# Merge units' maxima copied a slot later, the second weight sum in the next slot, weights asked for ahead of attention loads, and conv work paced by other counts

## The chip, the cores and the metric

The kernel runs on one core of a Trainium2 chip. Time is the device time of one execution in microseconds (us). The engines are TensorE (PE: matmuls and transposes; PEld are its weight loads), VectorE (DVE), ScalarE (ACT), GpSimd (POOL) and SyncE (SP), which here issues nearly all DMAs. Each engine works through its own queue in order and waits on semaphores for the others.

## What is computed

One decoder layer in float32 with a convolution branch and an attention branch, for x of 2048 tokens and 1024 channels. The attention has 12 heads of 128 channels in three dilated window groups, and four outputs are merged over the groups by a softmax of their log denominators.

```python
z = h @ w_in                                  # h: normalised x, 1024 -> 9728 columns
a, b, g_conv, q, k, v, g_attn, m_conv, m_attn = jnp.split(z, SPLIT_POINTS, axis=-1)
u = a * jax.nn.sigmoid(b)
u = depthwise_causal_conv(u, conv_w, conv_b)  # 31 taps
u = jax.nn.silu(layer_norm(u, conv_ln_w, conv_ln_b)) * jax.nn.silu(g_conv)
y_conv = u @ w_conv_out
q = rope(rms_norm(q, q_norm_w), positions)
k = rope(rms_norm(k, k_norm_w), positions)
...
o = jnp.sum(wts[..., None] * o.astype(jnp.float32), axis=0)   # merge over the groups
y_attn = (o * jax.nn.silu(g_attn)) @ w_attn_out
y = jax.nn.sigmoid(m_conv) * y_conv + jax.nn.sigmoid(m_attn) * y_attn
x = x + gate[:, None] * (y @ w_out)
```

## The kernel before

**The big product.** h @ w_in takes most of the time. The matrices are cut into quarters, and seven products take the place of eight (`PRODUCTS`: B11, B21, T2, T1, T3, B22, T4). T1 to T4 are sums of weight quarters. Every float32 operand is split into a high and a low part (names S_hi/S_lo, shT/slT, shB/slB: h is the high part, l the low one), and a product of four 128-row pieces is 4 x 3 = 12 matmuls. Such a product is a *slot*; its twelve matmuls follow each other every 0.23 us, 2.7 us together, while TensorE doesn't wait.

**The loop over slots** (L1597 on) does all of the work of the two token halves: first Q, K and V columns of half 0, then its gate columns, then the same for half 1 (`half_jobs`). In each slot it runs its agenda in a set order: enter, load, act, pe, vec, (prepare), act2, the product itself (with "mid" inside it), tail, store. TensorE's instructions stand in the order in which this loop writes them. DVE, ACT, POOL and SP stand so too in the stages of Q, K and V; from a few slots after the last V turn until the next half a scheduler orders them.

**Weights.** `column_steps` (L267 to L305): `load` asks for a weight quarter by a DMA on SP (L271), `combine` makes a sum on POOL (L276; T2 into a new tile wT2), `split` writes the high part on ACT (L281) and the low part on POOL or DVE (L282), and in half 0 it stores the sums T to DRAM (L287) for half 1, which loads them again. `prepare(s + AHEAD)` runs a split three slots ahead of its product, `ask(s + AHEAD + 2)` the loads five slots ahead.

**Rotation of K and Q.** After a K or Q column its sum of squares is taken (sqk, pssk, prqk), the inverse root is computed as a power on POOL (stk, L707: a tile of 128x16), set on ACT (L719) and finished on POOL (L723); TensorE spreads it over a matmul (pwk, L727), DVE makes rwk of it, and TensorE makes rsk (L736), which DVE multiplies in.

**Attention units.** `unit()` (L820 to L968) returns the steps of two query blocks with the slot in which each runs, counted from its scores: loads of q, k and v at -3 (`load`, L841 to L856, with "pkv", the earlier half's keys and values, where a unit crosses into it), the fetch of the merge's earlier partial sums at -1 under "store" in half 1 and at -2 under "load" in half 0 (L873), scores at 0, exponents at 1 (L901), the turn of the probabilities at 2 (ptp, then the copy pT by DVE in half 1 and by ACT in half 0, L913 to L915), weights of the merge at 3, values (po, L938), the output osb, its turn (pta, L959) at 5 and its store (L965) at 6. Units of group 0 (named 8_, 9_, 10_ and 11_ for the four heads) merge: they copy the other groups' maxima and sums into stm (POOL, L903), take the minimum (DVE), the exponents on ACT (L919) and DVE's products of them. The tags of the loads have few buffers: "x" (pkv and part) three, pT one.

**Conv work.** The 31-tap convolution runs on DVE in single steps (ce, cq) which the loop's end slips in as long as a credit lasts: each slot adds PACE for its stage and takes away `spent`, an estimate of what DVE was given in this slot (`Counted`, L206). All DVE instructions that go through `vec` bear the line L210. At the end of this loop "later" work of the start (xl, xs) is slipped in the same way.

## Time and profile before

| | us |
|---|---|
| three runs | 2369.66, 2358.53, 2369.1 |
| median | 2369.1 |
| the profiled execution | 2367.32 |
| its span | 2365.1 |

The profiled execution's mean granted TensorE clock was 0.992. How to read the views: a page's first part gives busy time, share of the span and number of instructions for each engine. Busy time by stretch gives, for each, its length, then busy time and instructions of PE, PEld, DVE, ACT and POOL, then the clock, the share of DMA and GB/s. The waits give who waited for whom, the total, the times and the longest. A timeline row is start, duration, engine, line, operation, and in brackets the idle time ahead of it and what ended it. Rows of groups give the line, engine, operation, out<-in, the shapes, the count, and the busy time and mean ns of one. Buffer numbers are left out of names there.

The stages on this clock: start-up to 65 us, Q, K and V of half 0 from there to about 290, attention of half 0 beside them and beside the gates to about 660, gates of half 0 to 960, Q, K and V of half 1 to 1470 with attention from 1130, its rest to 1580, gates of half 1 and the two output projections to 2365.

### The profile page before, as it was taken

How to read it: one execution, taken by the hardware profiler on the slowest of the kernel's cores; microseconds unless marked ns; L12 is line 12 of the kernel's file. 1: busy time of each engine (PE TensorE's matmuls, PEld its weight loads, DVE VectorE, ACT ScalarE, POOL GpSimd, SP SyncE). 2: the span in 40 equal slices, each digit the busy share in tenths (PEclk: the TensorE clock that was granted, in tenths of full speed). 3: DMA queues.
4: the chain of work that ended last, by engine and by line, in shares of the span. 5: the costliest groups of instructions: out<-in, count | busy, mean ns of one | idle time of the engine just before them, and what ended most of it. 6: DMA issues, size and time to landing. Idle time of an engine off the chain costs nothing. (4 is left out here: it accounts for less than half of the span.)

```text
span 2365.1 us, 34440 instructions
## 1 busy us (share of the span) xinstructions
PE 2293.5 (97%) x11434; PEld 1866.9 (79%) x11434; DVE 1716.0 (73%) x2826; ACT 1106.4 (47%) x2255; POOL 1107.1 (47%) x866
## 2 busy tenths in 40 slices
PE   6999899999999999999999999999999999999999
PEld 4777688887778888787788887877888888888887
DVE  6668664567969789858757557699997957787544
ACT  4744455556644444644544445544444444332221
POOL 2345444445577789955333343445566630000221
PEclk9999999999999999999999999999999999999999
DMA  7666556666554454543666665645444579865553
GB/s 265 194 217 227 180 174 202 207 211 192 171 185 156 157 188 172 186 125 114 192 185 187 208 190 186 210 157 186 137 139 148 170 251 327 289 230 193 178 161 103
DMA packets 301226, 446.29 MB, mean 189 GB/s; under 512 B 28916, under 2 KB 132468, under 8 KB 301048
## 3 DMA queue, kind: packets, MB, share of 16 engines
q1 hardware_dynamic: 286776, 418.38, 55.7%
q10 hardware_dynamic: 14272, 25.72, 2.9%
q8 instruction: 90, 1.47, 0.3%
q14 instruction: 88, 0.72, 0.1%
HBM read 282.88 MB, written 161.09 MB: 188 GB/s over the span
## 5 line engine op out<-in xcount | busy, mean ns | idle before, releaser
L282 POOL TENSOR_TENSOR slT<-wT,shT 128x512 fp32r<-128x512 f32 x172 | 234.7, 1365 | 289.5 <-ACT shT L281 274.6
L282 POOL TENSOR_TENSOR slB<-wB,shB 128x512 fp32r<-128x512 f32 x152 | 202.8, 1335 | 160.5 <-ACT shB L281 146.5
L281 ACT ACTIVATE shB<-wB 128x512 fp32r<-128x512 f32 x222 | 139.8, 630 | 175.7 <-issue 34.0
L282 POOL TENSOR_TENSOR slT<-wB,shT 128x512 fp32r<-128x512 f32 x98 | 131.3, 1344 | 142.2 <-ACT shT L281 130.6
L210 DVE SCALAR_TENSOR_TENSOR ce<-us,pair_taps,ce 128x512 f32<-128x512 f32 x240 | 180.8, 753 | 6.2
L210 DVE SCALAR_TENSOR_TENSOR ce<-ut,chan,ce 128x512 f32<-128x512 f32 x240 | 179.4, 747 | 0.5
L281 ACT ACTIVATE shT<-wT 128x512 fp32r<-128x512 f32 x176 | 110.4, 627 | 128.3 <-PE paab L344 22.3
L210 DVE SCALAR_TENSOR_TENSOR cq<-ut,chan,cq 128x512 f32<-128x512 f32 x208 | 155.3, 747 | 4.0 <-ACT cq L411 4.0
L210 DVE CUSTOM_DVE_ANT_0 sm<-ps,mask,rqq 128x256 f32<-128x256 f32 (+1 forms) x192 | 78.0, 443 | 82.2 <-PE ps L879 37.2
L276 POOL TENSOR_TENSOR wB<-wB,wB 128x512 f32<-128x512 f32 x80 | 110.7, 1384 | 47.8 <-DVE slB L210 42.4
L281 ACT ACTIVATE shT<-wB 128x512 fp32r<-128x512 f32 x120 | 75.3, 627 | 67.5 <-PE paab L344 30.9
L938 PE MATMUL po<-v,pT 128*128 128x128 f32 x560 | 81.9, 277 | 4.1 <-ACT pT L915 3.7
L139 POOL TENSOR_SCALAR stf<-stf 128x4 f32<-128x4 f32 x4 | 1.7, 414 | 179.5 <-DVE stf L1716 142.5
L938 PEld LDWEIGHTS po<-v,pT 128*128 128x128 f32 x560 | 75.2, 191 | 11.4 <-ACT pT L915 4.6
L1888 ACT ACTIVATE yh<-yq 128x512 fp32r<-128x512 f32 x48 | 27.3, 622 | 119.4 <-POOL yq L1882 45.0
L210 DVE TENSOR_TENSOR slB<-wB,shB 128x512 fp32r<-128x512 f32 x70 | 58.6, 839 | 28.0 <-ACT shB L281 24.9
L901 ACT ACTIVATE sm<-sm,osb 128x256 f32<-128x256 f32 (+1 forms) x128 | 58.5, 462 | 10.5 <-DVE osb L210 6.4
L1879 POOL TENSOR_TENSOR ys<-yq 128x512 f32<-128x512 f32 x8 | 11.1, 1393 | 98.8 <-DMA yq<-y_d 98.8
L276 POOL TENSOR_TENSOR wT<-wB,wB 128x512 f32<-128x512 f32 x40 | 54.9, 1374 | 2.3
L910 PE MATMUL ptp<-ident,sm 128*128 128x128 f32 x332 | 52.4, 274 | 3.4 <-DVE stm L210 3.0
L1947 DVE TENSOR_TENSOR xt<-xt,oa 128x512 f32<-128x512 f32 x32 | 22.0, 687 | 45.9 <-PE oa L1960 45.9
L910 PEld LDWEIGHTS ptp<-ident,sm 128*128 128x128 f32 x332 | 41.1, 140 | 17.7 <-issue 5.2
(893 smaller groups left out, 7867.2 us busy)
## 6 DMA issues: line engine op xcount, KB each, us to landing
wB<-in_w_in_dram SPq DMA_DIRECT2D x262, 256.0 KB, 4.0
wT<-tT_d SPq DMA_DIRECT2D x136, 256.0 KB, 2.9
tT_d<-wB SPq DMA_DIRECT2D x102, 256.0 KB, 3.5
qk<-qk_d SPq DMA_DIRECT2D x96, 256.0 KB, 3.9
v_d<-vev SPq DMA_DIRECT2D x48, 256.0 KB, 3.7
qk_d<-spare_hi SPq DMA_DIRECT2D x48, 256.0 KB, 4.1
qk_d<-spare_lo SPq DMA_DIRECT2D x48, 256.0 KB, 4.3
v<-v_d SPq DMA_DIRECT2D x96, 128.0 KB, 3.7
```

What stands on the lines that cost most here:

```text
L139: nc.gpsimd.tensor_scalar(scratch, src, EPS, None, op0=ALU.add)
L210: return f(out, *args, **kw)
L276: nc.gpsimd.tensor_tensor(dst, x0, x1, op=ALU.subtract)
L281: nc.scalar.activation(h, q[name], AF.Copy)
L282: eng.tensor_tensor(l, q[name], h.bitcast(F32), op=ALU.subtract)
L901: nc.scalar.activation(sm[:, a:z], sm[:, a:z], AF.Exp, scale=-1.0, bias=box["low"][i], accum_out=box["total"][i])
L910: nc.tensor.transpose(pt[:, c : c + P], box["sm"][:, c : c + P], ident)
L938: nc.tensor.matmul(po[:, P * i : P * i + P], box["pT"][:, c : c + P], vt, start=(m == 0), stop=(m == count[i] - 1))
L1879: pool_tt(s1, a21, a22, op=ALU.add)
L1888: nc.scalar.activation(h, src, AF.Copy)
L1947: add = lambda dst, ps: tc.keep_in_program_order(nc.vector.tensor_tensor(dst, dst, ps, op=ALU.add))
```

## The change

- The minima and copies of a merge unit (POOL's copy, DVE's minimum) become steps of their own in slot 2 instead of slot 1, and the minimum counts 0.5 more in `spent`.
- T2 is summed in the step of the next product (n == 1) instead of in that of the first.
- In half 1 the probabilities' copy pT goes to ACT as long as the slot is not behind the last V turn, to DVE after it.
- The fetch of half 1 runs in slot -1 under "load" instead of under "store".
- `ask`, the weights' loads, comes ahead of the "load" agenda in each slot.
- The conv allowance: PACE is higher in three stages, each counted DVE instruction costs 0.14 instead of 0.12, the splits of quarters that land (`landed`) count 0.4 each, and an extra rest (AFTER) is added in gate stages once no attention unit is left.

```diff
--- before.py
+++ after.py
@@ -39,7 +39,7 @@
 WS, WR, AHEAD = 4, 10, 3
 QKV_LO = (((1, 3, 5), (1, 3, 5), (0, 1, 3, 5, 6)), ((), (), (1, 3, 5)))
 FIRST_GATES, BETWEEN = (1, 1), ((1, 2, 1, 2, 1, 2, 1, 3), (1, 1, 2, 1, 1, 2, 1, 4))
-PACE, AGAIN = (2.75, 3.05, 2.5, 2.85), 12
+PACE, AFTER, AGAIN = (2.87, 3.15, 2.62, 2.85), (0.75, 0.1), 12
 PLAIN_QK, LATER_END = 4, 65
 MANUAL, ORDER_END = (True, True), 6
 LATER_X = 20
@@ -206,7 +206,7 @@
                 size = 1
                 for d in out.shape[1:]:
                     size *= d
-                spent[0] += 0.12 + size / 860 * (1.3 if name == "tensor_tensor" else 1.0)
+                spent[0] += 0.14 + size / 860 * (1.3 if name == "tensor_tensor" else 1.0)
                 return f(out, *args, **kw)
 
             return call
@@ -298,6 +298,7 @@
             split(PRODUCTS[n][1], vec if n in lo_engines else nc.gpsimd)
             if fresh and n == 0:
                 combine("T1", q["B11"], q["B12"], q["B11"])
+            if fresh and n == 1:
                 combine("T2", None, q["B22"], q["T1"])
             if fresh and n == 2:
                 combine("T3", q["B12"], q["B22"], q["B12"])
@@ -899,9 +900,15 @@
             for i in range(2):
                 a, z = cols[i][0], 256 * i + 256
                 nc.scalar.activation(sm[:, a:z], sm[:, a:z], AF.Exp, scale=-1.0, bias=box["low"][i], accum_out=box["total"][i])
+
+        def lows():
             if g == 0:
                 nc.gpsimd.tensor_copy(box["st"][:, 0:2, :, 1:NG], box["part"][:, :, :, P:].rearrange("p i g k -> p k i g"))
+
+        def lowest():
+            if g == 0:
                 vec.tensor_reduce(box["st"][:, 4, :, 0:1], box["st"][:, 0], op=ALU.min, axis=AX.X)
+                spent[0] += 0.5
 
         def turn_p():
             pt = bank("o", f"ptp{n}")
@@ -909,7 +916,7 @@
                 for c in cols[i]:
                     nc.tensor.transpose(pt[:, c : c + P], box["sm"][:, c : c + P], ident)
             pT = box["pT"] = ap.tile([P, 512], F32, tag="pT", name=f"pT{n}", bufs=1)
-            if half:
+            if half and slot_now[0] > last_v[1]:
                 vec.tensor_copy(valid(pT), valid(pt))
             else:
                 nc.scalar.activation(valid(pT), valid(pt), AF.Copy)
@@ -964,10 +971,10 @@
             if g == 0:
                 nc.sync.dma_start(ai_d[h, :, P * j0 : P * j0 + 2 * P], box["asb"])
 
-        return ((-3, "load", load), ((-1, "store", fetch) if half else (-2, "load", fetch)), (0, "pe", scores), (1, "act", exps), (2, "tail", turn_p), (3, "act", weigh),
+        return ((-3, "load", load), ((-1, "load", fetch) if half else (-2, "load", fetch)), (0, "pe", scores), (1, "act", exps), (2, "act", lows), (2, "vec", lowest), (2, "tail", turn_p), (3, "act", weigh),
                 (3, "tail", values), (4, "store", keep), (5, "pe", turn_o), (6, "store", keep_o))
 
-    waiting, busy_until = [], [0]
+    waiting, busy_until, last_v = [], [0], {}
     slots_of = {}
 
     opened(rb, pool("rb"))
@@ -1532,6 +1539,7 @@
     at_slot(where_of[half_jobs][0] + AGAIN, rope_again, "enter")
 
     last_turn = [slots_of[h, V, 5][6] for h in range(2)]
+    last_v.update(enumerate(last_turn))
 
     def order_shut():
         if order:
@@ -1594,6 +1602,10 @@
         at_slot(s + 42 + i, lambda i=i: gate_sum(i), "pe")
     at_slot(s + 44, lambda: aside.pop("gp_c").__exit__(None, None, None))
 
+    def landed(name, k, raw):
+        quarter_split(1, name, k, raw, nc.gpsimd if k == 3 else vec)
+        spent[0] += 0.4 * (k < 3)
+
     credit = 0.0
     for s, (i, n) in enumerate(slots):
         run_agenda(s, "enter")
@@ -1605,8 +1617,8 @@
             if last_turn[half] and s > last_turn[half] + 8 and not waiting and s > busy_until[0]:
                 last_turn[half] = 0
                 attention_shut()
+        ask(s + AHEAD + 2)
         run_agenda(s, "load")
-        ask(s + AHEAD + 2)
         for where in ("act", "pe", "vec"):
             run_agenda(s, where)
         prepare(s + AHEAD)
@@ -1624,10 +1636,11 @@
         for name, k in asked[:2]:
             raw = gpa["p"].tile([P, 512], F32, tag="ai" if k == 3 else "gt", name=f"landing{name}_{k}", bufs=2 if k == 3 else 6)
             nc.sync.dma_start(raw, quarter_src(name, k))
-            held.append((s + 3, lambda name=name, k=k, raw=raw: quarter_split(1, name, k, raw, nc.gpsimd if k == 3 else vec)))
+            held.append((s + 3, lambda name=name, k=k, raw=raw: landed(name, k, raw)))
         del asked[:2]
         stage = (i >= gates_start[0]) + (i >= half_jobs) + (i >= gates_start[1])
-        credit = min(max(credit, -2.0) + PACE[stage] - spent[0], 2.0)
+        rest = AFTER[i >= half_jobs] if not waiting and s > busy_until[0] and stage % 2 else 0.0
+        credit = min(max(credit, -2.0) + PACE[stage] + rest - spent[0], 2.0)
         spent[0] = 0.0
         while credit > 0.35 and (conv_todo or later_todo and s >= later_from.get(later_todo[0][0], s + 1)):
             if conv_todo:
```

The order of TensorE's instructions is the same row by row in both kernels. Line numbers of the kernel after are one higher from L301 on, three at POOL's copy of a part (L906) and seven from ACT's pT (L922) on.

POOL in half 0, at the columns from 5632, where K unit 0_1 is rotated; before:

```order
L707 TENSOR_TENSOR stk0_1_1895<-stk0_1_1895,mhalf_128 128x16
L282 TENSOR_TENSOR slB11_0_5632_1902<-wB11_0_5632_1823,shB11_0_5632_1901 128x512
L276 TENSOR_TENSOR wB11_0_5632_1823<-wB12_0_5632_1827,wB11_0_5632_1823 128x512
L276 TENSOR_TENSOR wT2_0_5632_1906<-wB22_0_5632_1829,wB11_0_5632_1823 128x512
L723 TENSOR_TENSOR stk0_1_1895<-stk0_1_1895 128x2x8
L282 TENSOR_TENSOR slT4_0_4096_1949<-wB21_0_4096_1662,shT4_0_4096_1948 128x512
L282 TENSOR_TENSOR slT2_0_5632_2007<-wT2_0_5632_1906,shT2_0_5632_2006 128x512
```

and now:

```order
L708 TENSOR_TENSOR stk0_1_1897<-stk0_1_1897,mhalf_128 128x16
L282 TENSOR_TENSOR slB11_0_5632_1904<-wB11_0_5632_1824,shB11_0_5632_1903 128x512
L276 TENSOR_TENSOR wB11_0_5632_1824<-wB12_0_5632_1828,wB11_0_5632_1824 128x512
L724 TENSOR_TENSOR stk0_1_1897<-stk0_1_1897 128x2x8
L282 TENSOR_TENSOR slT4_0_4096_1948<-wB21_0_4096_1663,shT4_0_4096_1947 128x512
L276 TENSOR_TENSOR wT2_0_5632_1980<-wB22_0_5632_1830,wB11_0_5632_1824 128x512
L282 TENSOR_TENSOR slT2_0_5632_2007<-wT2_0_5632_1980,shT2_0_5632_2006 128x512
```

The sum wT2 moved from ahead of the last step for stk0_1 (L723, now L724) to behind it and behind the low part slT4 of the column before.

In half 1, at the columns from 5376, the sum stood ahead of the power for stk1_0 (L707); now it stands behind that, behind the low part slT4 of the column before and behind the last step for stk1_0.

SP, the DMA queue, near the end of half 1's attention (qk, v and pkv are loads of unit 11_1_x, part of a merge unit, wT and wB weights, ai_d a store); before:

```order
L873 DMA part10_1_4_14894<-acc2_d_89 128x2x260
L844 DMA qk11_1_0_14946<-qk11_d_74 128x2x256
L852 DMA pkv11_1_0_14950<-qk11_d_74 128x128
L856 DMA pkv11_1_0_14950<-v11_d_86 128x128
L271 DMA wT4_1_128_15276<-tT4_128_d_6163 128x512
L965 DMA ai_d_97<-asb10_1_0_14966 128x256
L271 DMA wB11_1_8704_15319<-in_w_in_dram 128x512
L845 DMA v11_1_0_14947<-v11_d_86 128x256
L844 DMA qk11_1_2_15041<-qk11_d_74 128x2x256
L844 DMA qk11_1_4_15134<-qk11_d_74 128x2x256
L271 DMA wB21_1_8704_15364<-in_w_in_dram 128x512
L873 DMA part10_1_6_14995<-acc2_d_89 128x2x260
```

and now:

```order
L874 DMA part10_1_4_14858<-acc2_d_89 128x2x260
L845 DMA qk11_1_0_14948<-qk11_d_74 128x2x256
L874 DMA part10_1_6_14946<-acc2_d_89 128x2x260
L271 DMA wT4_1_128_15269<-tT4_128_d_6158 128x512
L972 DMA ai_d_97<-asb10_1_0_14964 128x256
L271 DMA wB11_1_8704_15314<-in_w_in_dram 128x512
L846 DMA v11_1_0_14949<-v11_d_86 128x256
L845 DMA qk11_1_2_15042<-qk11_d_74 128x2x256
L845 DMA qk11_1_4_15133<-qk11_d_74 128x2x256
L271 DMA wB21_1_8704_15354<-in_w_in_dram 128x512
L853 DMA pkv11_1_0_14952<-qk11_d_74 128x128
L857 DMA pkv11_1_0_14952<-v11_d_86 128x128
```

part10_1_6 moved up by nine rows, and pkv11_1_0 down behind the weight wB21_1_8704.

DVE at merge unit 8_1_2 in the last V columns (its two rows TENSOR_REDUCE are the minimum and, later, a sum); before, the minimum stands 13 rows ahead of the first row shown here:

```order
L210 TENSOR_TENSOR spare_lo_170<-s1v1_5_13907,pbv1_5_14035 128x512
L210 COPY pT8_1_2_14063<-ptp8_1_2_14058 128x512
L210 TENSOR_TENSOR stm8_1_2_13920<-stm8_1_2_13920 128x6
L210 TENSOR_REDUCE stm8_1_2_13920<-stm8_1_2_13920 128x2
L210 RECIPROCAL stm8_1_2_13920<-stm8_1_2_13920 128x2
L210 SCALAR_TENSOR_TENSOR stm8_1_2_13920<-stm8_1_2_13920 128x6
```

and now:

```order
L210 TENSOR_REDUCE stm8_1_2_13919<-stm8_1_2_13919 128x2
L210 TENSOR_TENSOR spare_lo_170<-s1v1_5_13907,pbv1_5_14035 128x512
L210 TENSOR_TENSOR stm8_1_2_13919<-stm8_1_2_13919 128x6
L210 TENSOR_REDUCE stm8_1_2_13919<-stm8_1_2_13919 128x2
L210 RECIPROCAL stm8_1_2_13919<-stm8_1_2_13919 128x2
L210 SCALAR_TENSOR_TENSOR stm8_1_2_13919<-stm8_1_2_13919 128x6
```

The copy pT8_1_2 is gone (ACT has it), and the minimum stands one row ahead of the product that needs ACT's exponent of it.

## The prediction

> **What bounds the kernel now.** I read the page first (busy shares), then busy time by stage, then the waits of TensorE, then the timeline at each wait. The page says that TensorE is the bound, and that almost nothing is left:
>
> ```profile
> PE 2293.5 (97%) x11434; PEld 1866.9 (79%) x11434; DVE 1716.0 (73%) x2826; ACT 1106.4 (47%) x2255; POOL 1107.1 (47%) x866
> ```
>
> The view of windows says in which stage TensorE is idle (the first number is the length, the second PE's busy time):
>
> ```profile
> 200.00:290.00 90.00, 77.50 (x380) 59.26 (x379) 67.45 (x89) 36.09 (x69) 44.64 (x31) 0.94 0.57 179
> 290.00:535.00 245.00, 243.41 (x1419) 199.60 (x1418) 142.47 (x296) 135.49 (x360) 113.82 (x83) 1.00 0.64 196
> 535.00:665.00 130.00, 120.84 (x643) 101.08 (x642) 114.11 (x280) 76.92 (x202) 73.07 (x74) 1.00 0.58 190
> 665.00:960.00 295.00, 295.00 (x1304) 244.25 (x1303) 247.72 (x360) 139.81 (x241) 248.30 (x198) 1.00 0.49 170
> 960.00:1130.00 170.00, 161.85 (x770) 130.34 (x769) 125.09 (x140) 90.22 (x154) 113.20 (x77) 0.98 0.45 138
> 1130.00:1470.00 340.00, 331.64 (x1909) 275.74 (x1907) 217.48 (x418) 163.71 (x399) 124.69 (x95) 1.00 0.62 187
> 1470.00:1560.00 90.00, 86.08 (x446) 72.14 (x445) 62.46 (x172) 50.16 (x132) 36.46 (x41) 0.96 0.66 210
> 1560.00:1660.00 100.00, 96.51 (x433) 78.92 (x432) 93.41 (x148) 44.05 (x83) 56.11 (x42) 0.98 0.54 173
> 1660.00:2365.00 705.00, 701.03 (x3066) 569.97 (x3064) 512.35 (x756) 255.71 (x433) 219.50 (x169) 1.00 0.60 194
> ```
>
> Length less busy time: 12.50, 1.59, 9.16, 0, 8.15, 8.36, 3.92, 3.49 and 3.97 us, 51.1 us after 200 us. The change keeps TensorE's own order and work, so all it can gain is a part of these, and the matmul time lost at half clock. The waits behind them:
>
> ```profile
> PE pta L959 <- DVE osb L210: 4.0, 2, 2.8
> PE po L938 <- ACT pT L915: 3.7, 2, 2.6
> PE rsk L736 <- DVE rwk L210: 3.5, 2, 2.2
> PE ptp L910 <- DVE stm L210: 3.0, 2, 1.6
> PE po L938 <- DVE pT L210: 2.6, 4, 1.0
> PE pssk L687 <- ACT sqk L668: 2.4, 1, 2.4
> ```
>
> (total, times, longest; those for stk are shown below one by one). The half clock, in four short windows round 206 us and two round 247 us (the last three numbers: granted clock, DMA share, GB/s):
>
> ```profile
> 202.70:206.10 3.40, 0.36 (x2) 0.00 (x0) 3.40 (x4) 0.00 (x0) 3.32 (x3) 1.00 0.00 0
> 206.10:209.50 3.40, 3.28 (x9) 2.60 (x10) 2.99 (x3) 0.29 (x1) 1.78 (x2) 0.50 0.03 5
> 209.50:212.90 3.40, 2.11 (x9) 1.18 (x8) 2.54 (x4) 1.22 (x2) 0.00 (x0) 1.00 0.77 189
> 212.90:216.30 3.40, 3.40 (x9) 2.66 (x9) 3.40 (x6) 0.76 (x2) 0.00 (x0) 0.50 0.96 270
> 243.60:247.00 3.40, 0.93 (x18) 0.45 (x18) 3.35 (x5) 1.69 (x3) 0.00 (x0) 1.00 0.46 100
> 247.00:250.40 3.40, 3.40 (x9) 2.63 (x10) 0.26 (x1) 2.11 (x4) 1.70 (x2) 0.51 0.92 276
> ```
>
> A window in which TensorE was idle for 3.04, 1.29 or 2.47 of 3.40 us is followed by 3.4 us at clock 0.50. Half of that, 1.7 us, is lost on top of the wait, so a wait of 2 to 3 us is worth up to 4 to 5. The stage rows agree: a mean clock of 0.94 in 90 us is 5.4 us lost, three times 1.7 and a rest; 0.98 in 170 us (960 to 1130) is 3.4, 0.96 in 90 (1470 to 1560) 3.6, 0.98 in 100 (1560 to 1660) 2.0.
>
> **The change part by part.**
>
> *Second weight sum (T2) a slot later.* In several QKV columns T2 stood on POOL ahead of steps that TensorE was about to wait for:
>
> ```profile
> 203.95 1.59 POOL L276 TENSOR_TENSOR wT<-wB,wB 128x512 f32<-128x512 f32 x1
> 204.34 1.75 DVE L210 TENSOR_TENSOR slB<-wB,shB 128x512 fp32r<-128x512 f32 x1
> 205.50 0.67 POOL L723 TENSOR_TENSOR stk<-stk 128x16 fp32r<-128x16 f32 x1
> 206.22 0.40 PE L727 MATMUL pwk<-ident,stk 128*32 128x128 f32 x1 [3.16 <-POOL stk L723]
> 211.34 0.66 DVE L210 TENSOR_TENSOR rwk<-pwk,edge 32x512 fp32r<-32x512 f32 x1
> 212.06 0.73 PE L736 MATMUL rsk<-rwk,pick 32*128 32x512 f32 x2 [1.29 <-DVE rwk L210]
> 1081.94 1.61 POOL L276 TENSOR_TENSOR wT<-wB,wB 128x512 f32<-128x512 f32 x1
> 1088.81 0.28 PE L727 MATMUL pwk<-ident,stk 128*32 128x128 f32 x1 [3.34 <-POOL stk L723]
> ```
>
> Near 206 us: stk moves up by one sum, 1.59 us, so pwk's wait goes from 3.16 to about 1.6 us. What is late next is rsk, which waits for rwk on DVE; rwk stands behind an addition whose input is the product that TensorE finishes after pwk. That product ran at half clock. If the 3.4 us at 0.50 go too, it ends 1.6 + 1.7 us earlier, but DVE's queue gives back about 1 of that. I take -2.2 (from 0, if rsk's wait grows by all of it, to -3.3). Near 1089 us the same swap is worth 1.61, and of the 3.4 us that this stage loses to the clock I put half to this wait: -2.5 (0 to -3.3). T2's own readers are a product later, so its delay is hidden by one slot (2.7 us).
>
> The Trainium skill has a rule on this cover. Its page "SBUF — State Buffer", section "Who interferes with whom", says that a VectorE operation with both inputs in SBUF and a GpSimd operation that reads SBUF exclude each other. The trace agrees in kind: DVE's slB took 1.75 us beside the sum. By this rule T2, put later, slows other DVE operations, perhaps those ahead of rwk. That is a rival below, where its price comes from the rows.
>
> *DVE's early work near 225 to 266 us.* Two "later" additions move into a stretch in which DVE idles:
>
> ```profile
> 225.02 1.09 DVE L210 TENSOR_TENSOR spare_lo<-s1k,pbk 128x512 f32<-128x512 f32 x1 [3.18 <-PE pbk L344]
> ```
>
> One (xl123) used to stand behind this wait of 3.18 us and now stands ahead of it, so the chain of DVE operations that runs on without a gap up to 246 us is one operation shorter: 0.93 us with POOL beside it, 0.74 without. pssk's 2.4 us wait shrinks to about 1.6; the half clock after it may go. I take -1.6 (0 to -2.6), and -0.7 for the same move of xl113 before 266 us.
>
> *pT copied by ACT in half 1 up to the last V turn.* 36 copies leave DVE and go to ACT:
>
> ```profile
> L915 ACT ACTIVATE pT<-ptp x48: 377/490/598, 280.5 to 648.7; 128x384 f32<-128x384 f32 x20, 128x256 f32<-128x256 f32 x16, 128x512 f32<-128x512 f32 x12
> L210 DVE COPY pT<-ptp x48: 670/684/714, 1128.3 to 1573.9; 128x512 f32<-128x512 f32 x48
> ```
>
> (minimum, median, maximum in ns). 36 x 0.684 = 24.6 us leave DVE; 36 x 0.6 = 21.5 us (the full width is the maximum of ACT's row) come on ACT, which has 164 us to do in the 340 of this stage where DVE has 217. Half 0, which copies on ACT already, is the nearest row for what results: 1.59 us idle in 245. Scaled to 340 us that is 2.2, against 8.36 now: -6.2 at most. Units of half 1 that merge have more to do than those of half 0 in that row, so I take half, -3, about what the four waits for DVE's pT come to (2.6). The other end is +1: a pT that waits for its transpose holds up ACT's split of a weight behind it.
>
> *Merge.* In half 1 the fetch of a merge unit's part goes half a slot ahead, and its copy and minimum a slot back. One place has a visible stall:
>
> ```profile
> 1528.64 0.19 POOL L903 COPY stm<-part 128x8 f32<-128x8 f32 x1 [2.51 <-DMA part<-acc_d]
> 1528.87 0.16 DVE L210 TENSOR_REDUCE stm<-stm 128x2 f32<-128x6 f32 x1 [1.98 <-POOL stm L903]
> ```
>
> This part is now asked for right behind unit 11_1_0's load of queries and keys; before, five more loads, three weights and a store came first. So the 1.98 us go; the keys and values of the earlier half for unit 11_1_0 (pkv) take the late place, a risk that belongs to the +4 below. Behind them DVE has no gap until TensorE has waited for it (the rows of L910 and L959 are of this place in part): directly it gets at most those 1.98 us back, and the clock's 3.6 us of this stage go or stay. Its row bounds it, 3.92 idle and 3.6: -7.5 to 0. Two conv steps moved ahead of this place by the new allowance fill a part of the time that comes free:
>
> ```profile
> L210 DVE SCALAR_TENSOR_TENSOR ce<-us,pair_taps,ce 128x512 f32<-128x512 f32 x240 | 180.8, 753 | 6.2
> ```
>
> I take -3.5: 0.5 to 2 of the idle time and about half of the clock's loss. The waits of 1560 to 1660 us, behind weights' landing and DVE at 93%, stay as they are: 0, at most their 3.5 and 2.0.
>
> *Weights asked ahead of loads, and the allowance.* SP issues the same transfers, 112 of them at another place. What is queued behind a weight that waits for its buffer is now an attention load:
>
> ```profile
> SPq L271 <- POOL slT L282: 137.1, 76, 3.8
> SPq L852 <- PE po L938: 90.8, 24, 10.6
> qk<-qk_d SPq DMA_DIRECT2D x96, 256.0 KB, 3.9
> ```
>
> The longest such wait is 3.8 us. A load is issued three slots of 2.7 us ahead of its scores and lands in 3.9, so some 4 us of cover hide it: 0, with +4 as the far end (a load late by one full wait). In return the weights no longer stand behind loads that wait up to 10.6 us. The allowance rises by as much as the new prices take, and in the gate stages the order of DVE is nearly the same: 0. One conv step (0.75 us, the row above) moves ahead of a split near 975 us whose result TensorE waits for, a part of the 8.15 us idle there: +0.75. The 2.6 us wait for ACT's pT and the rest of the 9.16 us of 535 to 665 keep their order: 0.
>
> *Sum:* -2.2 - 2.5 - 1.6 - 0.7 - 3 - 3.5 + 0.75 = -12.75, say -12. The profiled run took 2367.3 us (its span 2365.1); it becomes about 2355. The median of the three runs is 1.8 higher, so against it 2357.
>
> The Trainium skill's page "TensorE: Matmul & The Clock Gate", section "Why this matters for your kernels", warns of TensorE gaps of over about 3 us between bursts. The trace differs: 1.29 us idle in the window from 209.5 were enough. By that rule only the two pwk waits would cost clock; without the clock's part in pssk's and the merge's terms, some 2.4 us, the time would be 2359.
>
> **The rivals.**
>
> 1. *Given back at the next wait.* rsk waits for rwk on DVE, at 212 us and once more for 2.2, whatever pwk does, and a T2 that now runs beside DVE's operations makes them 1.75 instead of about 0.7 us long. Then the two pwk terms come to -1 together, pssk's stays as it is, and the attention gives -3: -4, or 2365. For it: the row of rwk; that DVE is in a row of operations there. Against it: the half clock goes with the wait.
> 2. *More than the sum.* All of the clock losses named (5.4, 3.4 and 3.6) and some of the 8.36 us go, with the direct terms: -20, or 2349. For it: half 0's 1.59 us. Against it: each such gain needs the next engine to be early too.
> 3. *Slower: the merge's exponent becomes the wait.* With the minimum a slot later, ACT's exponent of the maxima and DVE's product of it stand right behind it, where a slot lay between them:
>
> ```profile
> L919 ACT ACTIVATE stm<-stm x64: 279/286/298, 524.1 to 1565.9; 128x3 f32<-128x3 f32 x64
> ```
>
> DVE then stands still for two of these, 0.57, and for what ACT has in hand, some 0.6: 1.2 us for each of the 32 merge units (two rows each). It decides from where DVE has no slack left to take it. If the 16 of half 1 and a quarter of the others pass it on, 20 x 1.2 = +24, less what the QKV stages gain (6): +18, or about 2387. Against it: DVE is busy in 64% of 1130 to 1470.
> 4. *Nothing.* The moves lie where TensorE does not wait, the allowance undoes itself: 2369. Against it: two of the moved sums stand right before the longest waits.
>
> **How the numbers follow.** My forecast 0.42; rival 1 0.27; rival 2 0.15; rival 3 0.10; rival 4 0.06. About 0.5% (11.8 us, below 2357.3 or above 2381) is what a measurement of this kernel can tell from no change; the forecast lies on that bound, so half of its chance counts as faster. Faster: 0.21 + 0.15 + a little of the ends, 0.40. Slower: 0.10. Same: 0.50. The range takes in rival 1, 4 and most of rival 2: 2345 to 2372.
>
> **What would show it.** Right: pwk's waits near 206 and 1089 us are about 1.6 us, and the windows after them are at clock 1.00; no "DVE pT" among TensorE's waits before 1470 us; DVE's minimum near 1528 us doesn't wait for POOL. Wrong: rsk's waits grow by as much; new rows of TensorE waiting for ACT (pT, spare_hi) or for a DMA; DVE's stm waiting for ACT's exponent at many merges.

## The result, and the profile after

Over 16 runs the changed kernel takes 2357.45 us in the median (2352.97 to 2363.04), the kernel before 2366.92 (2358.53 to 2372.91) over 16: a ratio of 0.9964, interval 0.9953 to 0.9974. By the ratio that is 8.5 us less (6 to 11), while the two medians are 9.5 apart: faster beyond the interval, and short of 0.5%. The profiled execution of the changed kernel is its fastest run, 2352.97 us with a span of 2350.7 and a mean granted clock of 0.996; that of before took 2367.32 at 0.992. The two profiles are 14.4 us apart, and this is more than the kernels are: how much of it is clock comes below.

The page's first row, and busy time by the same stretches of the clock as before, in which the work stands up to 11 us earlier now (length, busy time of PE, PEld, DVE, ACT, POOL, then clock, DMA share, GB/s):

```profile
PE 2286.3 (97%) x11434; PEld 1863.7 (79%) x11434; DVE 1692.9 (72%) x2790; ACT 1121.6 (48%) x2291; POOL 1108.3 (47%) x866
...
200.00:290.00 90.00, 77.66 (x393) 59.81 (x392) 67.56 (x90) 38.06 (x71) 45.47 (x31) 0.96 0.61 194
535.00:665.00 130.00, 122.42 (x641) 102.34 (x640) 114.56 (x280) 77.51 (x203) 72.00 (x71) 0.99 0.62 199
960.00:1130.00 170.00, 162.72 (x794) 131.51 (x793) 126.19 (x143) 89.55 (x155) 118.12 (x78) 1.00 0.45 141
1130.00:1470.00 340.00, 334.23 (x1930) 279.62 (x1929) 193.10 (x393) 183.69 (x447) 124.13 (x93) 1.00 0.64 191
1470.00:1560.00 90.00, 86.75 (x455) 72.94 (x454) 70.77 (x189) 50.36 (x133) 39.24 (x42) 0.98 0.60 193
1560.00:1660.00 100.00, 98.15 (x436) 80.30 (x435) 94.20 (x134) 43.66 (x77) 59.09 (x44) 1.00 0.59 185
```

TensorE's idle time went from 12.50 to 12.34, 9.16 to 7.58, 8.15 to 7.28, 8.36 to 5.77, 3.92 to 3.25 and 3.49 to 1.85 us. DVE lost 23 us of work and ACT gained 15, which is pT. The clock's means are higher in four of the six stages (0.04 x 90 us lost in the first stretch instead of 0.06 x 90, nothing between 960 and 1130 instead of 3.4) and lower in one, from 535 to 665.

The waits of TensorE (total, times, longest) show what took the place of what:

```profile
PE rsk L737 <- DVE rwk L210: 6.2, 3, 3.2
PE pwk L728 <- POOL stk L724: 4.3, 3, 1.8
PE pta L966 <- DVE osb L210: 4.0, 2, 2.8
PE ptp L917 <- DVE stm L210: 2.5, 2, 1.5
PE pssk L688 <- ACT sqk L669: 2.3, 1, 2.3
PE po L945 <- ACT pT L922: 2.1, 2, 1.2
```

The wait for stk fell from 6.9 to 4.3, but that for rwk rose from 3.5 to 6.2: together 10.4 and 10.5. Waits for DVE's pT, 2.6 before, are down to one late one of 0.4.

### The profile page after: what moved, and what is told of

The parts are those of the page before. It is cut to its first block, busy times and chain, and to the rows that moved or that the text cites. A ratio compares the mean times of both kernels' runs of the same rounds, so it can differ in the third digit from the quotient of the medians.

```text
span 2350.7 us, 34465 instructions
## 1 busy us (share of the span) xinstructions
PE 2286.3 (97%) x11434; PEld 1863.7 (79%) x11434; DVE 1692.9 (72%) x2790; ACT 1121.6 (48%) x2291; POOL 1108.3 (47%) x866
## 3 DMA queue, kind: packets, MB, share of 16 engines
q8 instruction: 90, 1.47, 0.2%
## 4 chain that ended last, share of the span: by engine, by line
PE 51%; DVE 3%; DMA 2%; ACT 1%; issue 1%; POOL 0%; SPq 0%; ACTq 0%; DVEq 0%; POOLq 0%
PE yc L1691 8%; PE oa L1973 4%; PE ya L1691 4%; PE paab L345 3%; PE pak L345 3%; PE pav L345 3%; PE paq L345 2%; PE oc L1973 2%; PE pag_g_d L345 2%; PE pag_ma_d L345 2%; PE pcab L345 2%; PE po L945 2%; PE pcv L345 1%; PE pcq L345 1%; PE pck L345 1%; DMA wg<-in_w_ada_dram 1%
## 5 line engine op out<-in xcount | busy, mean ns | idle before, releaser
L922 ACT ACTIVATE pT<-ptp 128x512 f32<-128x512 f32 (+2 forms) x84 | 44.8, 533 | 90.3 <-PE ptp L917 90.1
L276 POOL TENSOR_TENSOR wB<-wB,wT 128x512 f32<-128x512 f32 x40 | 54.9, 1373 | 0.0
```

The lines of the kernel that those rows point to most:

```text
L276: nc.gpsimd.tensor_tensor(dst, x0, x1, op=ALU.subtract)
L922: nc.scalar.activation(valid(pT), valid(pt), AF.Copy)
```

## The experiments

**How they are read.** "Undone" is the changed kernel with that one part put back, "alone" is the kernel before with that part put in. All kernels have TensorE's order of before, row by row. Medians of 6 to 12 runs tell differences of some 3 us, and most terms are smaller; so each is read at its place in the profile as well. The runs' times go with the clock: the 16 runs of the changed kernel reach from 2352.97 us at 0.996 to 2363.04 at 0.992 and 2362.87 at 0.991. The table therefore also has the mean over runs of time x granted clock, roughly what a run takes without the half clock (time that TensorE idles at half clock is taken off too, so it is no exact split).

| kernel | median us | ratio to before (interval) | mean clock | time x clock | of before, run beside it |
|---|---|---|---|---|---|
| changed | 2357.45 | 0.9964 (0.9953-0.9974) | 0.9938 | 2343.1 | |
| changed, again | 2359.09 | 0.9967 (0.9951-0.9982) | 0.9928 | 2341.8 | 2349.1 |
| before, again | 2367.64 | 1.0002 (0.9988-1.0016) | 0.9918 | 2348.1 | 2349.1 |
| T2 undone | 2358.94 | 0.9972 (0.9956-0.9988) | 0.9928 | 2342.5 | 2349.2 |
| pT undone | 2360.5 | 0.9975 (0.9959-0.9992) | 0.9931 | 2344.9 | 2349.2 |
| weights' place undone | 2363.66 | 0.9985 (0.9968-1.0001) | 0.9922 | 2346.1 | 2349.2 |
| later minimum undone | 2359.99 | 0.9976 (0.9963-0.9990) | 0.9923 | 2342.8 | 2349.2 |
| earlier fetch undone | 2359.91 | 0.9974 (0.9964-0.9984) | 0.9922 | 2341.8 | 2349.7 |
| allowance undone | 2359.43 | 0.9976 (0.9964-0.9989) | 0.9925 | 2342.5 | 2349.7 |
| T2 and weights alone | 2363.95 | 0.9981 (0.9967-0.9996) | 0.9935 | 2348.1 | 2349.7 |
| pT alone | 2362.16 | 0.9991 (0.9978-1.0004) | 0.9923 | 2345.5 | 2348.2 |
| rotary operations back, all K columns | 2370.16 | 1.0009 (0.9999-1.0019) | 0.9911 | 2348.4 | 2349.7 |
| rotary operations back, one column | 2360.9 | 0.9975 (0.9962-0.9989) | 0.9923 | 2342.5 | 2349.1 |

**T2 undone.**

```diff
             if fresh and n == 0:
                 combine("T1", q["B11"], q["B12"], q["B11"])
-            if fresh and n == 1:
                 combine("T2", None, q["B22"], q["T1"])
```

> The changed kernel with T2 summed again in the step of the first product; all else as changed. My theory (T2's place on POOL is what shortened the waits near 541 and 1084 us): TensorE's wait for stk near 1084 us is 2.7 to 3.4 us again instead of 1.06, the wait for ACT's pT near 541 us is 2.0 to 2.6 instead of 0.93, near 206 us the wait for stk is 3 us and that for rwk behind it shrinks from 3.18 to about 1.5, so that nothing is lost or won there; time 3 to 6 us above the changed kernel. Rival (the gain near 541 us comes from the merge's later minimum, not from T2): the wait near 541 us stays at about 0.9 and the time is 2 to 4 us above.

TensorE's timeline near 207, 213 and 1093 us (in brackets the wait):

```profile
207.39 0.29 PE L727 MATMUL pwk<-ident,stk 128*32 128x128 f32 x1 [3.44 <-POOL stk L723]
212.97 0.73 PE L736 MATMUL rsk<-rwk,pick 32*128 32x512 f32 x2 [0.95 <-DVE rwk L210]
...
1093.02 0.28 PE L727 MATMUL pwk<-ident,stk 128*32 128x128 f32 x1 [2.72 <-POOL stk L723]
```

Near 207 us the pair comes to 4.4 us; in the changed kernel it is 1.84 + 3.18 = 5.0. Near 1093 the wait is back to 2.72 from 1.06. The median rose by 1.5 us only, and time x clock not at all (2342.5 against 2343.1 and 2341.8): less than expected, and less than 1.7 us at one place, since the waits for DVE behind it shrink again (for rsk and the sums of Q, from 1.62 us together to 0.41). Some 0.45 us are left of it there, and T2's move takes nearly as much back near 488 us: TensorE waits 0.61 us for sums of Q in the changed kernel and in its repeat, 0.22 with T2 undone and in both profiles of the kernel before. Near 547 us the wait for pT came out at 3.8 us, which seemed to bear out that T2 matters there, but see the repeats.

**pT undone, and pT alone.** One edit, taken from the changed kernel or put into the one before:

```diff
-            if half and slot_now[0] > last_v[1]:
+            if half:
                 vec.tensor_copy(valid(pT), valid(pt))
```

> The changed kernel with half 1's pT copied by DVE throughout. My theory (these 36 copies are what DVE lost between 1130 and 1470 us, and the stage's gain of 4 us is theirs): TensorE's idle time between 1130 and 1470 us rises from 5.8 to 8 or 9 us, with waits for DVE's pT and for DVE's sqq near 1150 and 1430 us again; time 2.5 to 4 us above the changed kernel. Rival (the later minimum of the merge and the earlier weights did it): that stage stays at 5.8 to 6.5 us idle and the time within 1 us of the changed kernel's.

> The kernel of before with half 1's pT copied by ACT up to the last V turn, nothing else. My theory (these copies alone are worth some 3 us, between 1130 and 1470 us, as undoing them gave 3 back there): the waits for DVE's pT near 1148, 1378 and 1430 us and for ACT's asb near 1443 us go, that stage's idle time falls from 8.36 us to 5 to 6, and the rest is as before; time 2 to 4 us below before. Rival (it takes the weights' earlier landing as well, since ACT waits in order): idle there 7 us or more, with new waits for ACT, time within 1 us of before.

The stage can be measured between two fixed matmuls: the first po with the earlier half's values (a row of the tile pkv gives the first and the last start) and the product pcv that waits 0.58 us near 1450 us. Before, changed, pT undone and pT alone, in this order:

```profile
L938 PE MATMUL po<-pkv,pT x104: 272/275/402, 1130.5 to 1550.9; 128*128 128x128 f32 x104
1452.88 0.50 PE L344 MATMUL pcv<-S_hi,shB 128*128 128x512 f32 x1 [0.58 <-DVE spare_lo L210]
```

```profile
L945 PE MATMUL po<-pkv,pT x104: 270/274/377, 1125.2 to 1539.8; 128*128 128x128 f32 x104
1443.56 0.50 PE L345 MATMUL pcv<-S_hi,shB 128*128 128x512 f32 x1 [0.58 <-DVE spare_lo L210]
```

```profile
L945 PE MATMUL po<-pkv,pT x104: 270/275/378, 1125.5 to 1541.2; 128*128 128x128 f32 x104
1446.84 0.50 PE L345 MATMUL pcv<-S_hi,shB 128*128 128x512 f32 x1 [0.58 <-DVE spare_lo L210]
```

```profile
L938 PE MATMUL po<-pkv,pT x104: 270/274/377, 1128.7 to 1544.8; 128*128 128x128 f32 x104
1447.76 0.50 PE L344 MATMUL pcv<-S_hi,shB 128*128 128x512 f32 x1 [0.58 <-DVE spare_lo L210]
```

From the one to the other it takes 322.4 us before, 318.4 changed, 321.3 with pT undone and 319.1 with pT alone. The repeats give 322.1 and 318.4, so this length is steady. pT is worth 2.9 us undone and 3.3 alone, and the medians go the same way (3.0 above the changed kernel; 4.0 below before, or 2 by the ratio, whose interval reaches 1.0004). TensorE's idle time in this stage fell by only 2.6 of the 4.0 us; the rest lies in rows that count as busy, above all those of po and of the products just ahead of a po.

The copies on ACT also cost something. Near 1193 us ACT's split of a weight now stands behind a pT, POOL's last step for stk comes later by it, and TensorE waits a microsecond longer. Before, and changed:

```profile
1199.99 0.29 PE L727 MATMUL pwk<-ident,stk 128*32 128x128 f32 x1 [0.41 <-POOL stk L723]
```

```profile
1193.22 0.28 PE L728 MATMUL pwk<-ident,stk 128*32 128x128 f32 x1 [1.42 <-POOL stk L724]
```

This wait is 0.40 or 0.41 us in all four profiles with pT on DVE, and 1.40 to 1.42 in all ten others. The 2.9 and 3.3 us are what is left with this cost in them.

**Weights behind the loads again.**

```diff
-        ask(s + AHEAD + 2)
         run_agenda(s, "load")
+        ask(s + AHEAD + 2)
```

> The changed kernel with the weights asked for behind the attention loads again. My theory (SP's order is covered by landings that come slots ahead): no stage's idle time changes by more than 0.5 us, time within 1 us. Rival (the weights' earlier landing frees POOL and ACT near 1090 to 1200 us and near 1620): idle time rises by 1 us or more in one of these stages, time 1 to 3 us above the changed kernel. Other rival (weights ahead of loads cost): time 1 to 3 us below.

The largest of the single steps: 6.2 us in the median, 3 to 4 by time x clock. The profile has new waits, 1.76 us for rwk near 354 us, 1.16 for stm near 1562, and 2.03 and 0.98 near 938 and 945 us. The last two are the chance event below, or follow it. The one for stm is no sign of the weights' place: it is there (1.16) with one rotary column moved too, where the program at this point is the changed kernel's. The one near 354 us stands in no other profile. What the weights' place does is seen on ACT, which splits them: its waits for a weight to land, before and with the place undone, in this order:

```profile
ACT shB L281 <- DMA wB<-in_w_in_dram: 7.7, 6, 2.7
```

```profile
ACT shB L281 <- DMA wB<-in_w_in_dram: 5.6, 4, 2.3
```

The repeat of the kernel before has 7.8 us in seven; neither profile of the changed kernel has this wait. Between the fixed matmuls of pT's stage, the place undone takes 319.1 us against 318.4, and the sums of Q near 1157 us wait 1.24 us instead of 0.52 (1.65 before). So the expectation of no effect does not hold: 0.7 us is shown at a steady place, and the wait near 354 us, 1.76, needs a second profile.

**The later minimum, and the earlier fetch, undone.** The first puts copy and minimum back into slot 1, the second is one word:

```diff
-        return ((-3, "load", load), ((-1, "load", fetch) if half else ...
+        return ((-3, "load", load), ((-1, "store", fetch) if half else ...
```

> The changed kernel with POOL's copy and DVE's minimum of a merge unit in slot 1 again, without the 0.5 counted for it; the earlier fetch stays. My theory (the stall near 1528 us goes with the earlier fetch, not with the later minimum): DVE's minimum near 1520 us waits for POOL by less than 0.5 us, the idle time of 1470 to 1560 us changes by less than 0.5; time within 1.5 us of the changed kernel. Rival (the later copy and minimum removed it): a DVE wait of 1 to 2 us for POOL's copy is back and the stage is idle for 1 to 2 us more.

> The changed kernel with half 1's fetch of the earlier partial sums in the store step again, half a slot later. My theory (the stall near 1528 us went by this earlier fetch): a DVE wait of 1 to 2 us for POOL's copy of a part is back near 1520 us and TensorE's idle time of 1470 to 1560 us rises from 3.25 to 4 or 5; time 0.5 to 3 us above the changed kernel. Rival (something else put it right, the weights' order or the later minimum): no such wait, time within 0.5 us.

With the fetch undone, the stall of before is back on POOL and DVE (timeline rows near 1524 us):

```profile
1524.54 0.19 POOL L906 COPY stm<-part 128x8 f32<-128x8 f32 x1 [2.40 <-DMA part<-acc_d]
1524.76 0.16 DVE L210 TENSOR_REDUCE stm<-stm 128x2 f32<-128x6 f32 x1 [1.87 <-POOL stm L906]
```

TensorE's idle time of 1470 to 1560 us is then 3.83 us, against 3.25 and, in the repeat, 3.17. With the minimum undone it is 3.09. So the fetch removes the stall, the later minimum does not, and the stall was worth 0.6 us to TensorE. It does not leave the stage without one: the minimum of a later unit, which didn't wait before, now does (1.43 us, and 1.55 in the repeat):

```profile
1539.03 0.16 DVE L210 TENSOR_REDUCE stm<-stm 128x2 f32<-128x6 f32 x1 [1.43 <-POOL stm L906]
```

Neither moves the median by more than it can tell.

**The allowance undone** (PACE, AFTER, 0.14 and what is counted for landings and minima as before):

> The changed kernel with the old conv allowance: the four old PACE values, no rest, 0.12 for an instruction, nothing counted for landings or for the merge's minimum. My theory (the allowance moves conv steps by one or two slots, where DVE is the late engine only from 1560 to 1660 us): that stage's idle time rises from 1.85 us towards 3.5, the others stay within 0.7; time 0 to 2 us above the changed kernel. Rival (the allowance does nothing): within 0.5 us everywhere. Other rival (it costs): 1 to 3 us below.

The stretch of 1560 to 1660 us got a wait of 3.32 us for ACT's spare_hi where the changed kernel had 0.93, but the repeat of the changed kernel has 2.43 there too. The time is within what a median tells. One place does show the allowance: with it undone a start-up addition (xl) is back behind DVE's wait of 3.2 us near 225 us, and pssk near 246 us waits 0.6 us longer. Changed, and undone:

```profile
245.72 0.94 PE L688 MATMUL pssk<-sqk,sel 128*32 128x128 f32 x16 [2.26 <-ACT sqk L669]
```

```profile
245.56 0.94 PE L688 MATMUL pssk<-sqk,sel 128*32 128x128 f32 x16 [2.87 <-ACT sqk L669]
```

The kernel of T2 and the weights alone, which has the old allowance too, waits 2.86; every other kernel with the new one 2.2 to 2.4.

**T2 and the weights' place alone, put into the kernel before.**

> The kernel of before with T2 a product later and the weights asked for ahead of the loads, nothing else. My theory (the wait near 545 us needs both, as undoing either brings it back): it falls from 2.56 to about 1 us, the waits for stk near 206 and 1089 us to 1.8 and 1.1, rsk's wait near 212 us grows to about 3; the waits for DVE's pT between 1130 and 1470 us stay; time 3 to 5 us below before. Rival (the later minimum is needed too): the wait near 545 us stays above 2 us and the time is 1 to 2 us below before.

pwk's waits are 1.49 and 1.09 us, rsk's 3.14, as in the changed kernel; po's is 0.55 near 545 us, though 1.31 us of waiting for osb stand ahead of it. The stage of pT is 320.7 us long: 1.7 of its 4 us come from these two edits, and they overlap with pT's 3.3. By time x clock the two are worth 1.6 us, by the median 2.

**Both kernels once more.**

> The changed kernel once more, as it is, to see what a second profile of the same program shows. My theory (the waits of one place are set by the program, the windows of half clock by where they happen to fall): the waits near 206, 212, 246, 270, 542, 655, 983, 1084 and 1193 us come out within 0.5 us, the wait of 0.93 us near 1609 us and the time lost to the clock do not (1.5 to 3 us and 4 to 14 us lost are possible); median within 2 us of 2357.5. Rival (the waits themselves vary by us from one execution to the next): several of them move by over 1 us.

> The kernel of before once more, as it is. My theory as for the changed kernel: its waits near 206, 246, 266, 271, 545, 985, 1089, 1148 to 1157 and 1430 to 1453 us are there again within 0.5 us, while the time lost to the clock differs by up to 6 us; ratio 1 within its interval.

In the changed kernel most waits came out within 0.2 us of the first profile, near 206, 212, 246, 1084 and through 1130 to 1470 us. In the kernel before so did most, but rsk's near 212 us is 0.63 instead of 1.29, and stk's near 1089 is 3.69 instead of 3.34. Other places moved by more, and three of them matter here. The wait for ACT's spare_hi, in the changed kernel, in its repeat, and before:

```profile
1608.57 0.50 PE L345 MATMUL pag_mc_d<-S_hi,shT 128*128 128x512 f32 x1 [0.93 <-ACT spare_hi L360]
```

```profile
1620.97 0.50 PE L345 MATMUL pag_mc_d<-S_hi,shT 128*128 128x512 f32 x1 [2.43 <-ACT spare_hi L360]
```

```profile
1622.19 0.50 PE L344 MATMUL pag_mc_d<-S_hi,shT 128*128 128x512 f32 x1 [2.46 <-ACT spare_hi L359]
```

So the fall from 2.46 to 0.93 is no gain of the change. Nor is that near 545 us: the repeat of the kernel before has no wait there at all:

```profile
541.83 1.16 PE L938 MATMUL po<-v,pT 128*128 128x128 f32 x8
```

The third is a new wait of 2.05 us near 935 us, in the repeat of the changed kernel. Its timeline shows one DVE operation of 4.77 us while POOL goes from one operation to the next:

```profile
927.37 4.77 DVE L210 SCALAR_TENSOR_TENSOR ut<-spare_hi 128x512 f32<-128x512 f32 x1
...
926.54 1.31 POOL L380 TENSOR_TENSOR spare_hi<-spare_hi 128x512 f32<-128x512 f32 x1
927.79 1.30 POOL L276 TENSOR_TENSOR wT<-wB,wB 128x512 f32<-128x512 f32 x1
929.04 1.31 POOL L276 TENSOR_TENSOR wB<-wB,wB 128x512 f32<-128x512 f32 x1
930.29 1.30 POOL L276 TENSOR_TENSOR wB<-wB,wT 128x512 f32<-128x512 f32 x1
...
935.48 0.65 PE L345 MATMUL pag_g_d<-S_hi,shT 128*128 128x512 f32 x1 [2.05 <-ACT spare_lo L360]
```

The operation ends 0.55 us after the last of the four POOL operations. The same operation took 0.73 us in the changed kernel's first profile, and 4.76 in those with the weights' place undone and with one rotary column moved, where TensorE waits 2.03 and 2.04 us behind it.

**Rotary operations behind rwk.** To see whether DVE's row ahead of rwk is what held rsk, two operations of that row were moved behind it: in all K columns of the other groups, then in the one near 206 us.

```diff
-            count = (2,) * 6
+            count = (2, 2, 2, 2, 0, 4) if which else (2,) * 6
```

> The changed kernel with two of DVE's rotary operations of a K column moved from the slot in which rwk is made to the next one, so that they stand behind rwk. My theory (T2's move gained nothing near 206 us because rwk stands behind a gapless row of DVE operations): rsk's waits near 212 and 269 us fall from 3.18 and 2.66 us to 1 to 1.5 each, the wait near 1193 us for stk stays; time 2 to 4 us below the changed kernel. Rival (rwk waits for ScalarE's copy of paq through the addition in front of it, not for DVE's row): rsk's waits stay within 0.5 us, time as changed.

> The changed kernel with the two rotary operations moved behind rwk in one K column only (pair 1 of half 0, near 206 us), and the next group's sine and cosine loaded one slot later there, so that they use the right table. My theory (near 206 us the gain of T2's move is stuck in DVE's row of operations ahead of rwk): rsk's wait near 212 us falls from 3.2 to about 1 us and the wait for stk before it stays at 1.5 to 1.9, the waits near 246 and 266 us are no longer; time 1 to 3 us below the changed kernel, by rows, and too little for the medians to tell. Rival (DVE gives it back at once): the waits behind it grow by as much, time as changed or above.

In the first, the next group's tables are loaded between, so some columns' last rotary products take another group's sine and cosine: that part of the computation is changed. Near 212 us rsk waits 0.81 us, near 269 us it still waits 3.14, and at other columns there are new waits (2.06 us near 492, 2.36 near 1157), and the time is 12.7 us above the changed kernel's. In the second:

```profile
195.04 0.75 DVE L210 SCALAR_TENSOR_TENSOR xl<-xl,mod,xl 128x512 f32<-128x512 f32 x1 [1.47 <-DMA h_d<-xl]
...
210.82 0.67 DVE L210 TENSOR_TENSOR rwk<-pwk,edge 32x512 fp32r<-32x512 f32 x1
...
211.54 0.73 PE L737 MATMUL rsk<-rwk,pick 32*128 32x512 f32 x2 [2.64 <-DVE rwk L210]
```

rsk's wait is 2.64 instead of 3.18: DVE had stood 1.47 us for a store of the start-up work and was 1.9 us later in its row (its product tmk starts at 205.78 instead of 203.85), which used up most of what the move saved. By itself 2.64 is no sign either way: in kernels whose program here is the changed kernel's, rsk waits 1.54 (pT undone) to 3.96 us (fetch undone). rwk does follow DVE's row, but a version that is faster did not come of it: 2360.9 against 2357.45 and 2359.09.

## Why the prediction was right, and where not

The time, 2357, came out (2357.45), and so did the range. The chances gave "within 0.5%" the most, 0.50, and that is where it ended. That the time was hit to half a microsecond is luck in part: the sum was -12, taken from a median of three runs, 2369.1; the gain is 8.5 to 9.5, from 2366.92 over 16 runs. The terms came out less evenly than their sum, and some were wrong in opposite ways.

- **T2 near 206 us: -2.2 forecast, nothing measured.** The step that failed is "DVE's queue gives back about 1 of that". It gave back all, and the half clock that I took off with it stayed: the windows from 210.7 to 217.5 us are at clock 0.50, as two windows there were before. The changed kernel's timeline:

```profile
204.90 0.67 POOL L724 TENSOR_TENSOR stk<-stk 128x16 fp32r<-128x16 f32 x1
207.25 1.74 POOL L276 TENSOR_TENSOR wT<-wB,wB 128x512 f32<-128x512 f32 x1
...
205.62 0.29 PE L728 MATMUL pwk<-ident,stk 128*32 128x128 f32 x1 [1.84 <-POOL stk L724]
211.82 1.22 PE L737 MATMUL rsk<-rwk,pick 32*128 32x512 f32 x2 [3.18 <-DVE rwk L210]
...
206.07 1.77 DVE L210 TENSOR_TENSOR slB<-wB,shB 128x512 fp32r<-128x512 f32 x1
207.76 1.77 DVE L210 SCALAR_TENSOR_TENSOR spare_lo<-spare_lo,hw,sin 128x512 f32<-128x512 f32 x1
211.09 0.67 DVE L210 TENSOR_TENSOR rwk<-pwk,edge 32x512 fp32r<-32x512 f32 x1
```

  pwk's wait is 1.3 us shorter, and rwk starts at 211.09 instead of 211.34 us. Before, DVE had 1.23 us to spare ahead of the addition in front of rwk (0.60 in the repeat), waiting for ACT; now it has none, and its row of operations, 8 us without a gap, sets when rwk comes. rsk's wait grew by 1.9 where pwk's fell by 1.3. That is the end which the first rival gave, but not shown to be for its reason: with T2 undone the row is as long (7.9 us) and also has two operations slowed to 1.75 and 1.76 us. Over the kernels with T2 moved and DVE's row left alone, the two waits together come to 3.2 to 5.2 us, and to 3.8 to 4.7 in those without: no gain at this place. The Trainium skill's "SBUF — State Buffer", section "Who interferes with whom", states that a DVE operation with two SBUF inputs and a GpSimd operation that reads SBUF exclude each other; here the trace agrees: slB takes 1.77 us beside POOL's slT and 0.70 with T2 undone, where it starts ahead of slT. No wait of the semaphores shows it, only the longer operation.

- **T2 near 1084 us: -2.5 forecast.** The wait fell by more than was worked out, from 3.34 to 1.06, and is 2.72 with T2 undone, so T2's own share, 1.66, came out. But rsk (0.39) and the sums of Q behind it (0.21, and 1.02 instead of 0.40), which wait for DVE, take back 1.2: the step that failed is that nothing behind this wait was charged. The direct part of the whole change is about -1 here, not -1.6, and T2 undone costs only 0.45 of it. The half clock that I put at 1.7 may have gone with it: all three profiles with neither T2 nor the weights moved have a half-clock window that starts between 1085 and 1091 us, and of the eleven others only that with the weights' place undone has one near (1100). That is too few to be sure.

- **The early DVE work: -2.3 forecast for pssk and 266 us, -0.7 measured.** pssk waits 2.26 (2.37 before), but TensorE now comes to it without the 0.6 us that it waited for pck near 238 us: the two together fell from 2.98 to 2.26, in the repeats from 3.01 to 2.26, and the allowance undone gives 0.6 back. That is the direct part that was forecast for the first addition. The half clock behind it is in one of the changed kernel's two profiles and in both of before. For the second addition, the 0.5 us won at pcv near 264 us are lost at rsk (2.66 instead of 2.19).

- **pT: -3 forecast, -3.3 alone and -2.9 undone.** The size came out, but it was worked out as idle time, and idle time fell by 2.0 alone and 1.6 undone: the halving of the scaled figure was a guess that fitted. What I put as the far end of +1, a split of a weight held up on ACT, is there as a wait of 1.0 us near 1193 us, inside this sum.

- **Merge: -3.5 forecast.** The mechanism is right: the fetch removes the stall. The size is off: 0.6 us of idle time. The rest was to come from the clock, and the half-clock windows of this stage vary between profiles whether the stall is there or not (two and one before, one in each profile of the changed kernel, one with the fetch undone).

- **Weights: 0 forecast.** Here the term was mis-sized the other way. Undone it costs 6.2 us in the median, of which chance has a part; alone with T2 it gains 1.6 to 2. The cover that I named hides the loads, but I gave the weights' own earlier landing nothing, and ACT had stood 7.7 us for it. How much it brings is left open between about 1 and 4 us.

- **A conv step ahead of a split near 975 us: +0.75 forecast, not shown.** TensorE's wait for that split, near 985 us, is 3.00 and 3.73 us in the changed kernel's two profiles, 2.98 and 3.08 before.

- **Waits near 545 and 1622 us: 0 forecast.** They fell by 1.6 and 1.5 us in the profile, but the repeats show that this is chance: right, and it would have looked wrong from two profiles.

- **The clock.** Time x clock gives 2349 before and 2342 to 2343 after: some 6.7 us of the 8.5 are direct, and they are near the sum of what the stages show: 4.0 from 1130 to 1470, about 1 near 1084, 0.7 from 1470 to 1560 and 0.7 near 238 to 246 us, less 0.4 near 488 us. What is left, 2 us or less, may be fewer windows at half clock (mean 0.9938 and 0.9928 against 0.9918 to 0.9927), which these runs cannot tell from nothing. In the two profiles the clock differs by 0.004 (0.9924 and 0.9956, 18.0 and 10.2 us lost), which is 7.8 us of the 14.4, less what TensorE waited in those windows. My sum treated lost windows as belonging to waits; a wait raises their chance, but a profile shows one draw.

The second rival (more than the sum) and the third did not come: TensorE's waits for stm between 1470 and 1560 us shrank (ptp's from 1.59 to 1.02 us), and DVE's waits for ACT's exponents are 14.1 us in all, 14.2 before, so the exponent that now stands right behind the minimum is no new bound. The fourth, nothing, is outside the interval.

## What to carry to other kernels

When a wait is shortened, look at what the next wait hangs on: where two queues feed one chain, moving work out of one of them gains no more than the other has to spare. Before explaining small differences between two profiles, profile each kernel twice: what repeats belongs to the program, the rest to the draw. Where idle time is down to 2 or 3%, a steady gain is read between two fixed instructions more surely than from whole times.

## What the runs showed that was not expected

- The clock is a draw of each execution: the same program ran at a mean of 0.990 to 0.996, and its times go with it, 2352.97 us at 0.996 and 2362.87 at 0.991. The Trainium skill's "TensorE: Matmul & The Clock Gate", section "What's actually happening", says that the window over which the clock gate watches TensorE's activity is free-running and is not reset when a kernel starts; runs that differ in their lost windows, while their waits repeat, agree with that.
- One DVE operation took 4.77 us instead of 0.73 while POOL operations followed each other without a gap, and it ended with them, in the repeat of the changed kernel and not in its first profile, which is the same program. It reached TensorE as a wait of 2.05 us; DVE was busy for 14.86 of the 15 us from 920 us in the first profile, so it has little to spare there. That POOL held it is the likely cause, read from the times alone.
